# The values products of a dilated attention stage: one product of 128 columns for both halves of v, two PSUM banks for each block

## The chip, the cores and the metric

The kernel runs on one core of a Trainium2 chip. The core has a matrix engine (TensorE, PE in the profile, with its weight loads shown as PEld), a vector engine (VectorE, DVE), an activation engine (ScalarE, ACT), a general engine (GpSimd, POOL) and a queue that issues transfers (SyncE, SP). The matrix engine writes only into PSUM, a memory of eight banks of 512 float32 values for each of 128 partitions; DVE and ACT read results out of it, POOL does not in this kernel. The metric is the device time of one execution in microseconds, lower is better, as the median of several runs.

## The reference, cut to what matters

An encoder layer runs over two sequences, of 2048 and of 512 tokens. A projection of the normed input gives queries, keys and values for a 2-D neighbourhood attention and for three dilated attentions (dilations 1, 4 and 16), and gates. The change is in the dilated attentions: each query sees its neighbours within half a window in a subsequence of stride `dil`.

```python
def band_attention(q, k, v, half):      # per subsequence, blocks of queries
    ...
    s = jnp.einsum('bnqhd,bnkhd->bnhqk', qp, kw).astype(jnp.float32) / math.sqrt(dh)
    s = jnp.where(ok[:, None], s, NEG)
    m = jnp.max(s, axis=-1, keepdims=True)
    p = jnp.exp(s - m)
    den = jnp.sum(p, axis=-1, keepdims=True)
    o = jnp.einsum('bnhqk,bnkhd->bnqhd', (p / den).astype(v.dtype), vw)
    lse = (m + jnp.log(den))[..., 0].transpose(0, 1, 3, 2)
    ...
for gi, (win, dil) in enumerate(((128, 1), (512, 4), (2048, 16))):
    o, lse = dilated_attention(q, k, heads(parts[base + 2]), win, dil)
wts = jax.nn.softmax(jnp.stack(lses), axis=0)
o_b = jnp.einsum('gblh,gblhd->blhd', wts, jnp.stack(outs))
```

There are 8 heads of 64 values. All inputs are float32.

## The kernel before

**Two halves for each number.** Float32 accuracy is had from 16-bit products: a number is split into a high and a low 16-bit part, and a product of two numbers is made as high by low, high by high and low by high, all added in PSUM. Projections, scores and values all work so.

**Stages.** The dilated stage comes first, then the neighbourhood stage, then the gates, then the output. In the dilated stage the kernel goes through 60 tiles of 128 tokens, 20 for each dilation. For each tile it makes three projections (q, k, v), each of 24 products of 512 columns into one of four PSUM banks `proj` (`bank`, line 699). ACT copies q or k out of the bank (`qk<-proj`) and squares it out of the bank (`sq<-proj`, after which the bank is free), DVE adds up the squares (`q_ssq`), POOL turns and scales the result, ACT and DVE or POOL split it into halves (`qs`), and a transfer turns it. ACT and DVE split v into `dv`, in which the 64 high and the 64 low parts of a head stand side by side.

**A block of attention** (`dil_block`, line 1533) is 128 or 64 queries against one or two tiles of 128 keys. There are 66 blocks: 30 with 256 keys and 36 with 128. The eight heads are dealt to units: with 256 keys four units of two heads (0 and 2, 1 and 3, 4 and 6, 5 and 7), with 128 keys two units of four heads (the even ones, the odd ones). Units go in pairs. For each unit PE makes scores into one of two banks `s`; DVE adds the mask and takes each row's maximum in one instruction (`e<-s,cmask`, printed as ISA in the lists of order below) and writes the maximum into the block's tile `osb`; ACT turns it into a shift (`neg<-osb`), makes the exponential and its sum; ACT or DVE round it to `p`, DVE or POOL make the low part; a transfer turns p into `pT`.

**The values** (`pump`, line 854) come when a unit's `pT` has landed, in the order of the units. For each head and tile of keys there are three products with 64 columns of v, each with its own weight load of a 128-column piece of `pT`: high p by low v, high p by high v, low p by high v. With 256 keys that is 48 products for a block, with 128 keys 24. All eight heads of a block, 64 columns each, go into one bank `o`; the kernel has two such banks, so that consecutive blocks alternate. After the last unit `finish` copies 512 columns from the bank to `osb` on ACT, gives the bank back, and `store` writes `osb` to memory and frees the block's q and v tiles. The neighbourhood stage uses the same `pump` and the same two banks.

**What sets the order.** The program is written out by a planner in the kernel itself. It keeps a clock (`Clock`) and a queue for each engine, books a cost for each instruction (`mm`, `act`, `vec`, `pool`), and emits what is ready next. `copy` and `either` choose ACT or DVE, DVE or POOL, by which would be done first by the booked costs. PE's order is the projections, with scores and values put in at the moment when the planner's clock says that their inputs are there and, for the values, that a bank `o` has been granted (`Slots`). Each engine then executes its own list in this order.

Of the kernel before, what the change touches and what calls it, by code (L numbers as in the profile page):

```python
# [18 lines left out]
ALU = mybir.AluOpType  # L19
# [62 lines left out]
M_S = 0.0  # L82
# [92 lines left out]
class Slots:  # L175
# [89 lines left out]
class Enc:  # L265
# [588 lines left out]
    def pump(self):  # L854

        while self.values and "ready" in self.values[0]:
            u = self.values[0]
            if u["first"] and "o" not in u["st"]:
                u["st"]["o"] = None

                def granted(u=u):
                    u["st"]["o"] = self.new("o", [128, 512])
                    self.pump()

                self.S["o"].take(granted)
                return
            if u["st"].get("o") is None or len(u["v"]()) < u["n"] // 128:
                return
            self.values.popleft()
            m, nch, nh = u["m"], u["n"] // 128, len(u["hs"])  # L870
            for i, h in enumerate(u["hs"]):
                out = u["out"](i)
                for j in range(nch):
                    v = u["v"]()[j][:, h]
                    ph, pl = (u["pT"][:, c * nch * nh + i * nch + j, :m] for c in range(2))
                    self.mm(out[:m], ph, v[:, 1], j == 0, False)
                    self.mm(out[:m], ph, v[:, 0], False, False)
                    self.mm(out[:m], pl, v[:, 0], False, j == nch - 1)
            self.S["pT"].give(u["pT"])
            if "last" in u:  # L880
                self.clk.then(u["last"])
# [231 lines left out]
    def na_group(self, seq, g):  # L1113
# [50 lines left out]
        def unit(c, hs):  # L1164
# [4 lines left out]
            u = {"m": 128, "n": n, "hs": hs, "first": hs[0] == 0, "v": lambda: st["v"], "sc": self.sc[0], "st": st,  # L1169
                 "bm": bm}  # L1170

            def scores(s):
# [19 lines left out]
                return st["den"][:, hs[j]:hs[j] + 1]  # L1192

            def out(j):
                return st["o"][:, 64 * hs[j]:64 * hs[j] + 64]

            def finish():
                osb = st["osb"] = self.new("osb", [128, 256], pool=self.N["osb"])
                st["parts"] = self.N["osb"].tile([128, 2, 256], FP16, name=f"oparts{S['osb'].index(osb)}", bufs=1)
                rden = self.T.tile([128, 4], F32, name="rden")  # L1200
                self.vec("reciprocal", rden, st["den"])
                self.vec("tensor_tensor", osb.rearrange("p (h d) -> p h d", d=64),
                         st["o"][:, 0:256].rearrange("p (h d) -> p h d", d=64),
                         rden.unsqueeze(2).to_broadcast([128, 4, 64]), op=ALU.mult)
                S["o"].give(st["o"])
                S["vc"].give(st["vt"])
                clk.then(high)

# [324 lines left out]
    def dil_block(self, R, srcs, m, q, ks, vs, mask, free):  # L1533
# [6 lines left out]
        def unit(h0):  # L1540

            hs = tuple(range(h0, h0 + 2 * nh, 2))

            def scores(s):
                return [(s[:m, n * j:n * j + n], q(), self.ring[:, :, ks()], h, 8, m) for j, h in enumerate(hs)]

            def osb():
                if "osb" not in st:
                    st["osb"] = self.new("osb", [128, OW])
                return st["osb"]  # L1550

            def finish():
                self.act(st["osb"][:m, 0:512], st["o"][:m])
                S["o"].give(st["o"])
                clk.at(clk.done + M_S, store)

            def store():
                p0 = 0
                for t, cnt in srcs:
                    cnt = min(cnt, m)  # L1560
                    self.dma(self.rows_of(self.ob_d[gi], t, cnt, d), st["osb"][p0:p0 + cnt])
                    p0 += cnt
                S["osb"].give(st["osb"])
                free()
                self.blocks_left -= 1
                if self.blocks_left == 0:
                    self.dil_done.signal()

            u = {"m": m, "n": n, "hs": hs, "first": h0 == 0, "st": st, "v": vs, "scores": scores, "sc": self.sc[1],
                 "scored": lambda: None,  # L1570
                 "mask": lambda j: mask, "topped": lambda: None, "out": lambda j: st["o"][:, 64 * hs[j]:64 * hs[j] + 64],
                 "mx": lambda: osb()[:m, 512 + h0:511 + h0 + 2 * nh:2], "den": lambda j: osb()[:m, 520 + hs[j]:521 + hs[j]]}
            if hs[-1] == 7:
                u["last"] = finish
            return u

# [599 lines left out]
```

## Time and profile before

| what | value |
|---|---|
| median of 3 runs | 2861.87 us (2861.65 to 2867.31) |
| profiled execution, its own time | 2864.63 us |
| its span, first to last instruction | 2862.8 us |
| mean granted TensorE clock | 0.971 of full speed |
| busy: PE, DVE, ACT, POOL | 93%, 55%, 47%, 52% of the span |
| dilated stage | from the start to about 1263 us |
| neighbourhood stage | about 1263 to 1800 us |
| gates and output | from about 1800 us |

The table's shares are means over stages that differ. Two stretches of the dilated stage are read apart in the rows below: 140 to 870 us, in which the blocks of dilations 1 and 4 end (39 evacuations of `o`), and 870 to 1263 us. A PE instruction's length in the profile holds its passage through the array, and consecutive ones overlap; what a product takes of PE's time is read from the distance between starts. "idle before" of a group is the time that the engine stood still ahead of those instructions, with what ended it.

### The profile page before, as it was taken

How to read it: one execution, taken by the hardware profiler on the slowest of the kernel's cores; microseconds unless marked ns; L12 is line 12 of the kernel's file. 1: busy time of each engine (PE TensorE's matmuls, PEld its weight loads, DVE VectorE, ACT ScalarE, POOL GpSimd, SP SyncE). 2: the span in 40 equal slices, each digit the busy share in tenths (PEclk: the TensorE clock that was granted, in tenths of full speed). 3: DMA queues.
4: the chain of work that ended last, by engine and by line, in shares of the span. 5: the costliest groups of instructions: out<-in, count | busy, mean ns of one | idle time of the engine just before them, and what ended most of it. 6: DMA issues, size and time to landing. Idle time of an engine off the chain costs nothing.

```text
span 2862.8 us, 55914 instructions
## 1 busy us (share of the span) xinstructions
PE 2675.4 (93%) x20841; PEld 1788.6 (62%) x20841; DVE 1576.5 (55%) x3670; ACT 1334.6 (47%) x3561; POOL 1474.7 (52%) x1991
## 2 busy tenths in 40 slices
PE   5998989989999999999898886899999999999999
PEld 2444444444444444455455554889999999999887
DVE  7777666775655764557676687332145444454111
ACT  5666666665666665656666667221123121122010
POOL 4987768677778888756676664000012121131110
PEclk9999999999999999999999996899999999999999
DMA  7999886766675755588998897332144344353443
GB/s 208 223 214 195 176 196 110 158 127 119 114 121 114 156 114 115 98 224 182 192 226 190 180 206 169 85 71 75 45 129 159 109 128 133 110 172 118 148 139 110
DMA packets 808017, 419.21 MB, mean 146 GB/s; under 512 B 689728, under 2 KB 734400, under 8 KB 801344
## 3 DMA queue, kind: packets, MB, share of 16 engines
q1 hardware_dynamic: 807744, 415.63, 62.9%
q8 instruction: 163, 2.67, 0.4%
q14 instruction: 110, 0.90, 0.1%
HBM read 171.72 MB, written 79.13 MB: 88 GB/s over the span
## 4 chain that ended last, share of the span: by engine, by line
PE 65%; DVE 9%; POOL 8%; DMA 7%; ACT 6%; issue 4%; SPq 1%; DVEq 0%; POOLq 0%; ACTq 0%
PE proj L352 54%; PE s L352 10%; POOL qk L377 4%; DMA pT<-p 4%; PE o L352 2%; DVE p L365 2%; ACT e L360 2%; DVE e L365 2%; POOL sq L377 2%; DMA qn<-qs 1%; POOL q_t L377 1%; ACT sq L360 1%; DVE wm L365 1%; DVE q_ssq L365 1%; ACT qk L360 1%
## 5 line engine op out<-in xcount | busy, mean ns | idle before, releaser
L352 PEld LDWEIGHTS <-hb 128*128 128x128 f16 x6240 | 591.6, 99 | 684.6 <-issue 124.8
L352 PE MATMUL proj<-wt,hb 128*128 128x512 f16 (+2 forms) x3360 | 688.0, 357 | 26.1 <-ACT sq L360 18.0
L352 PE MATMUL proj<-wu,hb 128*128 128x512 f16 x2880 | 668.4, 385 | 45.1 <-ACT sq L360 30.5
L360 ACT ACTIVATE sg<-proj,wi 128x256 f32<-128x256 f32 x240 | 113.1, 473 | 639.3 <-PE proj L352 629.7
L360 ACT ACTIVATE e<-e,neg,sc 128x256 f32<-128x256 f32 (+4 forms) x688 | 393.4, 574 | 8.4 <-DVE neg L365 4.5
L352 PE MATMUL proj<-hb,wt 128*128 128x256 f16 x2760 | 313.7, 274 | 5.0 <-DMA hb<-htd 2.1
L352 PEld LDWEIGHTS <-pT 128*128 128x128 f16 (+1 forms) x4560 | 227.7, 102 | 139.1 <-DMA pT<-p 64.1
L352 PEld LDWEIGHTS <-wt 128*128 128x128 f16 x2760 | 269.3, 98 | 39.4 <-issue 4.0
L377 POOL TENSOR_TENSOR qk<-qk,sq 128x512 f32<-128x512 f32 (+1 forms) x141 | 183.9, 1304 | 196.2 <-DVE qk L365 100.7
L365 DVE TENSOR_TENSOR p<-e,p 128x512 f16<-128x512 f32 (+2 forms) x278 | 248.1, 893 | 63.4 <-ACT p L360 59.6
L377 POOL TENSOR_TENSOR sq<-qk,gcs 128x256 f32<-128x256 f32 x240 | 191.4, 818 | 135.6 <-DVE q_ssq L365 128.9
L365 DVE TENSOR_TENSOR qk<-s,sg 128x256 f32<-128x256 f32 x160 | 67.7, 424 | 348.1 <-PE s L352 345.6
L352 PE MATMUL s<-hb,wt 128*128 128x256 f32 x1880 | 246.9, 285 | 0.0
L352 PE MATMUL proj<-hb,kT 128*128 128x256 f16 x1920 | 228.2, 276 | 5.2 <-ACT sg L360 2.7
L352 PEld LDWEIGHTS s<-hb,wt 128*128 128x128 f32 x1880 | 231.2, 189 | 0.9
L377 POOL TENSOR_TENSOR hb<-sg,hb 128x256 fp32r<-128x256 f32 x65 | 54.0, 831 | 341.3 <-ACT hb L360 341.3
L365 DVE CUSTOM_DVE_ANT_0 e<-s,cmask 128x256 f32<-128x256 f32 (+2 forms) x528 | 154.3, 344 | 107.1 <-PE s L352 90.2
L352 PEld LDWEIGHTS <-kT 128*128 128x128 f16 x1920 | 184.4, 99 | 30.5 <-DVE kT L365 3.5
L365 DVE CAST p<-e 128x512 f16<-128x512 f32 (+2 forms) x182 | 120.1, 660 | 131.4 <-ACT e L360 109.5
L377 POOL TENSOR_TENSOR qk<-qk,q_y 128x512 f32<-128x512 f32 x160 | 179.2, 1124 | 5.2
L377 POOL TENSOR_TENSOR qk<-qk,gcs 128x512 f32<-128x512 f32 x120 | 167.0, 1391 | 9.4
L352 PE MATMUL proj<-wv,hb 128*128 128x512 f16 x660 | 156.6, 383 | 8.3 <-ACT sq L360 6.9
(181 smaller groups left out, 3774.9 us busy)
## 6 DMA issues: line engine op xcount, KB each, us to landing
hb<-htd SPq DMA_DIRECT2D x40, 1024.0 KB
wr<-in_w_in SPq DMA_DIRECT2D x132, 256.0 KB
obd<-osb SPq DMA_DIRECT2D x50, 264.0 KB
hd<-xs SPq DMA_DIRECT2D x20, 512.0 KB
htd<-hb SPq DMA_DIRECT2D x10, 1024.0 KB
mad<-qk SPq DMA_DIRECT2D x40, 256.0 KB
e<-obd SPq DMA_DIRECT2D x40, 256.0 KB
sq<-mad SPq DMA_DIRECT2D x40, 256.0 KB
```

What stands on the lines that cost most here:

```text
L352: self.nc.tensor.matmul(out, a, b, start=start, stop=stop, **kw)
L360: self.nc.scalar.activation(out, x, func, **kw)
L365: getattr(self.nc.vector, ins)(out, *a, **kw)
L377: getattr(self.nc.gpsimd, ins)(out, *a, **kw)
```

## The change

In the dilated stage, high p now meets the low and the high part of v in one product: the 128 columns of a head in `dv` are taken whole, and the result is 128 columns wide, 64 of high p by high v and 64 of high p by low v. Low p by high v follows with 64 columns and is added to the first half. So a head and tile of keys takes two products and two weight loads in place of three. Four heads of 128 columns fill a bank, and a block of eight heads takes both banks `o`. With 256 keys the first two units fill one bank and the last two the other; with 128 keys each unit writes to both. When the last odd unit of a bank has been done, ACT copies the second halves (256 columns) to `osb`, DVE adds the first halves out of the bank, and the bank is given back; after both, the block is stored. The neighbourhood stage keeps its products and one bank for a block.

```diff
@@ pump @@
-            if u["first"] and "o" not in u["st"]:
-                u["st"]["o"] = None
...
+            o = u["st"].setdefault("o", {})
+            for b in u["banks"]:
+                if b not in o:
+                    o[b] = None
+
+                    def granted(o=o, b=b):
+                        o[b] = self.new("o", [128, 512])
+                        self.pump()
+
+                    self.S["o"].take(granted)
+                    return
+                if o[b] is None:
+                    return
...
-                    self.mm(out[:m], ph, v[:, 1], j == 0, False)
-                    self.mm(out[:m], ph, v[:, 0], False, False)
-                    self.mm(out[:m], pl, v[:, 0], False, j == nch - 1)
+                    if u["wide"]:
+
+                        self.mm(out[:m], ph, v.rearrange("p x d -> p (x d)"), j == 0, False)
+                        self.mm(out[:m, 0:64], pl, v[:, 0], False, j == nch - 1)
+                    else:
...
@@ dil_block @@
+            banks = sorted({h // 4 for h in hs})
+
...
             def finish():
-                self.act(st["osb"][:m, 0:512], st["o"][:m])
-                S["o"].give(st["o"])
-                clk.at(clk.done + M_S, store)
+                for b in banks:
+                    out = st["osb"][:m, 256 * b:256 * b + 256].rearrange("p (h d) -> p h d", d=64)
+                    o = st["o"][b][:m].rearrange("p (h x d) -> p h x d", x=2, d=64)
+                    self.act(out, o[:, :, 1])
+                    clk.then(add, b, out, o[:, :, 0])
+
+            def add(b, out, o):
+                self.vec("tensor_tensor", out, out, o, op=ALU.add)
+                S["o"].give(st["o"][b])
+                st["left"] = st.get("left", 2) - 1
+                if st["left"] == 0:
+                    clk.at(clk.done + M_S, store)
...
-            if hs[-1] == 7:
+            if hs[-1] % 2:
                 u["last"] = finish
```

Over the whole program the lists of instructions differ in this: 2304 products of 64 columns become 768 of 128 and 768 of 64, with 768 weight loads fewer; ACT's 66 copies of 512 columns become 132 of 256; DVE has 132 additions of 256 columns more. The planner's choices move a little too: DVE rounds 10 pieces of p more and ACT 10 fewer (8 of 128x512), ACT makes 12 shifts `neg` of dilated units more and DVE 12 fewer, POOL makes 8 low parts of p more.

**DVE where a block ends and the next one's scores begin**, some 700 us into the stage. `q_ssq` is the sum of squares of a projection, `dv` the low part of v, `qs` and `p` halves, the tile behind `o` in a row is a bank of values, and the ISA row is the mask and maximum of the next block's first unit. Before:

```order
L365 CAST p1_8735<-e1_8693 128x512
L365 TENSOR_TENSOR qs0_8723<-qk2_8519,qs0_8723 128x512
L365 TENSOR_REDUCE q0_ssq_8760<-sq1_8727 128x8
L365 TENSOR_REDUCE q1_ssq_8819<-sq0_8799 128x8
L365 ISA e0_8859,osb0_8860<-s0_8838,cmask_302 128x256
```

Now:

```order
L365 TENSOR_TENSOR p1_8460<-e1_8421,p1_8460 128x512
L365 TENSOR_REDUCE q2_ssq_8491<-sq0_8479 128x8
L365 TENSOR_TENSOR osb0_8130<-osb0_8130,o1_8392 128x256
L365 TENSOR_TENSOR osb1_8313<-osb1_8313,o0_8482 128x256
L365 SCALAR_TENSOR_TENSOR dv0_8557<-proj0_7670,dv0_8557 128x8x64
L365 TENSOR_TENSOR osb1_8313<-osb1_8313,o1_8538 128x256
L365 ISA e0_8605,osb0_8606<-s0_8588,cmask_302 128x256
```

Three additions of two blocks stand ahead of the next block's mask and maximum, where before there were none.

**ACT at the same place.** `osb<-o` is the evacuation, `neg` the shift for the next block's first unit, which needs DVE's maximum. Before:

```order
L360 ACTIVATE sq0_8799<-proj0_8731 128x512
L360 ACTIVATE q1_y_8821<-q1_ssq_8819,wi4_976 128x8
L360 ACTIVATE q1_y_8821<-q1_y_8821,lnq_184 128x8
L360 ACTIVATE neg0_8861<-osb0_8860,sc1_316 128x2
L360 ACTIVATE neg1_8866<-osb0_8860,sc1_316 128x2
L360 ACTIVATE e0_8859,osb0_8860<-e0_8859,neg0_8861,sc1_316 128x256 x2
L360 ACTIVATE e1_8865,osb0_8860<-e1_8865,neg1_8866,sc1_316 128x256 x2
L360 ACTIVATE osb1_8591<-o1_8743 128x512
```

Now:

```order
L360 ACTIVATE sq0_8479<-proj3_8417 128x512
L360 ACTIVATE osb0_8130<-o1_8392 128x256
L360 ACTIVATE q2_y_8493<-q2_ssq_8491,wi4_976 128x8
L360 ACTIVATE q2_y_8493<-q2_y_8493,lnq_184 128x8
L360 ACTIVATE osb1_8313<-o0_8482 128x256
L360 ACTIVATE dv0_8557<-proj0_7670 128x8x64
L360 ACTIVATE osb1_8313<-o1_8538 128x256
L360 ACTIVATE neg0_8607<-osb0_8606,sc1_316 128x2
L360 ACTIVATE neg1_8612<-osb0_8606,sc1_316 128x2
L360 ACTIVATE e0_8605,osb0_8606<-e0_8605,neg0_8607,sc1_316 128x256 x2
```

The evacuation has moved from behind the next block's shifts and exponentials to ahead of them, in two pieces, with a third of the block before.

**PE where one block's values follow another's**, some 960 us into the stage: the last product of a block, then projections (`proj<-wu,hb`), then the next block's first product. Before (63 projection products lie between the two blocks):

```order
L352 MATMUL o0_12437<-dv1_12033,pT5_12405 128x64
L352 LDWEIGHTS hb0_11935
L352 MATMUL proj2_12499<-wu23_7637,hb0_11935 128x512
...
L352 LDWEIGHTS pT0_12659
L352 MATMUL o1_12776<-dv2_12239,pT0_12659 128x64
```

Now (6 lie between):

```order
L352 MATMUL o1_12132<-dv1_11565,pT5_12068 128x64
L352 LDWEIGHTS hb0_11451
L352 MATMUL proj1_12186<-wu14_6485,hb0_11451 128x512
...
L352 MATMUL proj1_12271<-wu15_6917,hb0_11451 128x512
L352 LDWEIGHTS pT0_12123
L352 MATMUL o0_12261<-dv2_11838,pT0_12123 128x128
L352 LDWEIGHTS pT0_12123
L352 MATMUL o0_12261<-dv2_11838,pT0_12123 128x64
```

Before, the next block writes to the other bank. Now it writes to the banks that the block before it has just filled. Of the 130 times that a bank is used again in the dilated stage, 9, at 6 places, have 15 or fewer projection products between its last product and its next one: 6, 12, 12, 15, 15 and 15. Before, the fewest between two uses of one bank were 51.

## Rows read from the trace of the kernel before

**Rows 1.** Page: busy time, share of the span and instructions of each engine.

```profile
PE 2675.4 (93%) x20841; PEld 1788.6 (62%) x20841; DVE 1576.5 (55%) x3670; ACT 1334.6 (47%) x3561; POOL 1474.7 (52%) x1991
```

**Rows 2.** Windows: stretch, length, busy us of PE, PEld, DVE, ACT, POOL; clock, DMA.

```profile
140.00:870.00 730.00, 666.34 (x5052) 329.64 (x5053) 486.81 (x1188) 471.05 (x1309) 558.69 (x756) 0.97 0.77 151
870.00:1263.00 393.00, 387.01 (x2814) 193.69 (x2813) 223.57 (x635) 232.32 (x718) 319.46 (x474) 0.99 0.62 128
```

**Rows 3.** PE's groups, 140 to 870 us: count | busy us, mean ns | idle before, releasers.

```profile
L352 PE MATMUL proj<-wu,hb 128*128 128x512 f16 x1197 | 284.2, 387 | 29.1 <-ACT sq L360 28.5 <-DVE dv L365 0.3 <-DVE wm L365 0.2
L352 PE MATMUL proj<-wt,hb 128*128 128x512 f16 x780 | 185.5, 386 | 13.4 <-ACT sq L360 11.2 <-DVE dv L365 2.2
L352 PE MATMUL proj<-wv,hb 128*128 128x512 f16 x480 | 114.1, 384 | 8.3 <-ACT sq L360 6.9 <-DVE dv L365 1.3
L352 PE MATMUL o<-dv,pT 128*128 128x64 f16 x1392 | 60.9, 195 | 1.1 <-DMA pT<-p 1.1
L352 PE MATMUL o<-dv,pT 128*64 128x64 f16 x252 | 11.9, 198 | 2.4 <-DMA pT<-p 2.4
L356 PE MATMUL proj<-ident,wm 128*1 128x128 f32 x5 | 1.5, 292 | 5.8 <-ACT sq L360 5.8
```

**Rows 4.** The same, 870 to 1263 us.

```profile
L352 PE MATMUL proj<-wu,hb 128*128 128x512 f16 x1253 | 283.6, 380 | 2.0 <-ACT sq L360 2.0
```

**Rows 5.** Waits, 140 to 870 us: engine <- releaser: us in total, times, longest.

```profile
ACT neg L360 <- DVE osb L365: 124.5, 97, 6.7
...
PE proj L352 <- ACT sq L360: 46.7, 23, 5.8
...
PE proj L356 <- ACT sq L360: 5.8, 3, 2.3
```

**Rows 6.** Tiles qk and osb, 140 to 870 us: count, ns min/median/max, first and last start.

```profile
L360 ACT ACTIVATE qk<-proj x69: 570/577/597, 140.1 to 865.9; 128x512 f32<-128x512 f32 x69
...
L360 ACT ACTIVATE osb<-o x39: 570/576/598, 161.0 to 867.4; 128x512 f32<-128x512 f32 x29, 64x512 f32<-64x512 f32 x10
```

**Rows 7.** Timeline of PE: start us, us, what, x how many in a row.

```profile
701.23 1.46 PE L352 MATMUL proj<-wu,hb 128*128 128x512 f16 x6
702.52 0.51 PE L352 MATMUL o<-dv,pT 128*128 128x64 f16 x12
702.87 0.81 PE L352 MATMUL proj<-wu,hb 128*128 128x512 f16 x3
...
704.16 0.51 PE L352 MATMUL o<-dv,pT 128*128 128x64 f16 x12
...
706.55 0.56 PE L352 MATMUL o<-dv,pT 128*64 128x64 f16 x12
707.05 2.76 PE L352 MATMUL proj<-wt,hb 128*128 128x512 f16 x12
```

**Rows 8.** Page: weight loads of the attention's values, whole span.

```profile
L352 PEld LDWEIGHTS <-pT 128*128 128x128 f16 (+1 forms) x4560 | 227.7, 102 | 139.1 <-DMA pT<-p 64.1
```

**Rows 9.** ACT's groups, whole span: evacuations of 512 and of 256 columns.

```profile
L360 ACT ACTIVATE osb<-o 128x512 f32<-128x512 f32 x54 | 31.4, 582 | 24.2 <-PE o L352 24.1
L360 ACT ACTIVATE v<-proj 128x256 f16<-128x256 f32 x40 | 15.0, 374 | 21.2 <-DMA vd<-v 20.1 <-PE proj L352 1.0
L360 ACT ACTIVATE osb<-o 64x512 f32<-64x512 f32 x12 | 6.9, 576 | 0.0
```

**Rows 10.** DVE's group of the same form as the new additions, whole span.

```profile
L365 DVE TENSOR_TENSOR osb<-o,rden 128x256 f32<-128x256 f32 x40 | 17.0, 424 | 14.4 <-PE o L352 11.1
```

**Rows 11.** POOL's dearest subtraction, 100 to 1200 us.

```profile
L377 POOL TENSOR_TENSOR p<-e,p 64x512 f16<-64x512 f32 x3 | 10.9, 3636 | 1.3 <-DVE p L365 1.3
```

**Rows 12.** Timelines of PE and ACT: a block's last products, its evacuation; another's evacuation.

```profile
985.09 0.51 PE L352 MATMUL o<-dv,pT 128*128 128x64 f16 x12
...
991.71 0.58 ACT L360 ACTIVATE osb<-o 128x512 f32<-128x512 f32 x1
...
704.72 0.60 ACT L360 ACTIVATE osb<-o 128x512 f32<-128x512 f32 x1 [2.46 <-PE o L352]
```

More of the change, by code (lines that the diff above doesn't have):

```diff
@@ L857, in pump @@
             u = self.values[0]
-            if u["first"] and "o" not in u["st"]:
-                u["st"]["o"] = None
[L861 to L867, printed above, removed]
+            o = u["st"].setdefault("o", {})
[9 more added lines that the diff above has]
+                    return
+            if len(u["v"]()) < u["n"] // 128:
                 return
@@ L875, in pump @@
                     ph, pl = (u["pT"][:, c * nch * nh + i * nch + j, :m] for c in range(2))
-                    self.mm(out[:m], ph, v[:, 1], j == 0, False)
-                    self.mm(out[:m], ph, v[:, 0], False, False)
-                    self.mm(out[:m], pl, v[:, 0], False, j == nch - 1)
+                    if u["wide"]:
+                        self.mm(out[:m], ph, v.rearrange("p x d -> p (x d)"), j == 0, False)
+                        self.mm(out[:m, 0:64], pl, v[:, 0], False, j == nch - 1)
+                    else:
+                        self.mm(out[:m], ph, v[:, 1], j == 0, False)
+                        self.mm(out[:m], ph, v[:, 0], False, False)
+                        self.mm(out[:m], pl, v[:, 0], False, j == nch - 1)
             self.S["pT"].give(u["pT"])
@@ L1168, in unit @@
             bm = [bms[(0, 1, 1, 2)[c], h] for h in hs]
-            u = {"m": 128, "n": n, "hs": hs, "first": hs[0] == 0, "v": lambda: st["v"], "sc": self.sc[0], "st": st,
+            u = {"m": 128, "n": n, "hs": hs, "banks": [0], "wide": False, "v": lambda: st["v"], "sc": self.sc[0], "st": st,
                  "bm": bm}
@@ L1194, in out @@
             def out(j):
-                return st["o"][:, 64 * hs[j]:64 * hs[j] + 64]
+                return st["o"][0][:, 64 * hs[j]:64 * hs[j] + 64]
             def finish():
@@ L1202, in finish @@
                 self.vec("tensor_tensor", osb.rearrange("p (h d) -> p h d", d=64),
-                         st["o"][:, 0:256].rearrange("p (h d) -> p h d", d=64),
+                         st["o"][0][:, 0:256].rearrange("p (h d) -> p h d", d=64),
                          rden.unsqueeze(2).to_broadcast([128, 4, 64]), op=ALU.mult)
-                S["o"].give(st["o"])
+                S["o"].give(st["o"][0])
                 S["vc"].give(st["vt"])
@@ L1552, in finish @@
             def finish():
-                self.act(st["osb"][:m, 0:512], st["o"][:m])
-                S["o"].give(st["o"])
-                clk.at(clk.done + M_S, store)
+                for b in banks:
[9 more added lines that the diff above has]
+                    clk.at(clk.done + M_S, store)
             def store():
@@ L1567, in store @@
                     self.dil_done.signal()
-            u = {"m": m, "n": n, "hs": hs, "first": h0 == 0, "st": st, "v": vs, "scores": scores, "sc": self.sc[1],
+            u = {"m": m, "n": n, "hs": hs, "banks": banks, "wide": True, "st": st, "v": vs, "scores": scores, "sc": self.sc[1],
                  "scored": lambda: None,
-                 "mask": lambda j: mask, "topped": lambda: None, "out": lambda j: st["o"][:, 64 * hs[j]:64 * hs[j] + 64],
+                 "mask": lambda j: mask, "topped": lambda: None, "out": lambda j: st["o"][hs[j] // 4][:, 128 * (hs[j] % 4):128 * (hs[j] % 4) + 128],
                  "mx": lambda: osb()[:m, 512 + h0:511 + h0 + 2 * nh:2], "den": lambda j: osb()[:m, 520 + hs[j]:521 + hs[j]]}
-            if hs[-1] == 7:
+            if hs[-1] % 2:
                 u["last"] = finish
```

## The prediction

> **What bounds the kernel now.** I read the page first, then two windows of the dilated stage, then PE's groups in each, the waits, and last single rows. PE is busy for 93% of the span, the others for about half [rows 1]. The two stretches differ [rows 2]: from 140 to 870 us PE is busy for 666.3 of 730 us, from 870 to 1263 us for 387.0 of 393. So in the second nothing but PE's own work counts, and in the first 64 us stand open. What opens them is one thing: PE's projections wait for a bank, and the bank is freed by ACT's `sq`, 28.5 + 11.2 + 6.9 us of such waits, and 5.8 us in the small transposes of the weights' scales [rows 3], in all 52.4 us. The waits view counts 23 for the first 46.7 us and 3 for the other 5.8 [rows 5]: 26 waits, where ACT empties 69 banks of q and k [rows 6]: about 4 in 10 (26/69 = 0.38) come too late. After 870 us such waits make 2.0 us [rows 4]. Why is ACT late? Its longest wait is for DVE: 124.5 us, 97 times, ahead of `neg`, until DVE has a unit's maxima [rows 5]. DVE and ACT wait for each other in turn, each in its fixed order, and PE feels it when four banks don't cover it. No engine of the three is full: DVE is busy for 487 of the 730 us, ACT for 471, POOL for 559 [rows 2].
>
> **What is removed on PE.** A third of the loads and products. What is that worth? Twelve products of 64 columns run from 702.52 to the next product at 702.87 us: 0.35/12 = 29 ns each [rows 7]. Six of 512 columns run from 701.23 to 702.52: 215 ns each. The difference, 186 ns for 448 columns, is 0.415 ns for a column, which is the 2.4 GHz level (0.417), so a product costs 2.3 ns beside its columns. The weight load that each has takes 102 ns as a row [rows 8], but it does not show in the distance: it is done under the products before it. The three products have 192 columns, and so have the two: 128 + 64. The wide one should take 29 + 64 x 0.415 = 55.6 ns, the pair 84.6 in place of 87. That saves 2.4 ns, 768 times: 1.8 us. With 64 queries twelve products take 0.50 us to the next [rows 7], a little more, but these are an eighth of all (288 of 2304), and I take -2 us for the whole. The bounds: no gain at all if the wide product is slower than its columns, and at most a third of the time in which values products keep PE busy (60.9 + 11.9 us in the first stretch [rows 3], 24 us or so after it), about -32 us.
>
> The Trainium skill, "TensorE: Matmul & The Clock Gate", section "Back-to-back issue gap", says that in a stream of pairs of load and product the distance is about 81 ns for 128 columns and about 131 ns for 512. By its 81 ns the pair would take 110 ns in place of 87, and the sum would be some 18 us higher. For 512 columns this trace has 215 ns and not 131, so I don't take it; no row of this trace has a load and a product of 128 full columns.
>
> **What is added on DVE and ACT.** 132 additions of 128 (or 64) x 256. The nearest row is the neighbourhood stage's product out of the same kind of bank, 424 ns [rows 10]: 56.0 us. On ACT 66 evacuations of 582 or 576 ns go (38.3 us), and 132 of 256 columns come, nearest row 374 ns [rows 9], 49.4 us: +11.1 us. All of it lies beside PE, so its cost is what reaches PE by ACT's late `sq`. In the first stretch 39 blocks are evacuated [rows 6]: 78 additions, 33.1 us, and 39 x (2 x 0.374 - 0.58) = 6.6 us on ACT, together 39.7 us. The lowest value is 0: DVE stands still for a third of that stretch. The highest is all 39.7. Between them: an added time can reach PE only at those banks where PE waits already, 0.38 of them, which gives 15.0 us. I take half of that, 7.5 us, because half of each chain of waits is ACT waiting for DVE and half DVE waiting for ACT, and an addition lengthens a queue only where DVE isn't waiting itself. After 870 us I take 0: PE hardly waits there, and ACT and DVE are busy for less than 0.6 of it.
>
> The queues behind the new instructions: an addition waits for ACT's copy, and behind it on DVE stand, as the order shows, `dv` (which frees a projection's bank) or the next block's mask and maximum, for which ACT's `neg` waits. The copies move ahead of the next block's `neg` on ACT, so there the old lateness of the evacuation falls, and that of `neg` grows. The moved choices are small: 10 roundings of p go from ACT to DVE, and POOL gets two more of a dear form, 3.6 us each [rows 11]; POOL has 170 us open in the stretch, and p lands well ahead of its products (PE waits 1.1 + 2.4 us for `pT` [rows 3]). I cost them at 0. `store` comes about 0.8 us later for each block; it holds one of two tiles `osb`, but a block comes every 18 us or so (39 in 730 us [rows 6]), so this too is 0; if the neighbourhood's start hung on the last block it would be those 0.8 us, once.
>
> **The new wait: the bank.** Before, a block had the other bank while its predecessor was read out. Now PE's first product of a block stands behind the addition that empties the bank, in PE's fixed order. The planner leaves 6, 12, 12, 15, 15 and 15 projection products at the six tightest places: 1.3, 2.6, 2.6, 3.2, 3.2 and 3.2 us at 215 ns. How long does emptying take? ACT begins a block's evacuation between 0.05 us (704.16 + 0.51, then 704.72 [rows 7, 12]) and 6.1 us (985.60, then 991.71 [rows 12]) after the last product; over the 66 pairs of such rows the median is 1.5 us. Then come two copies of 0.374 and one addition of 0.424, and DVE may be at something else, which I estimate at 1 us from its busy share of two thirds and its instructions of 0.4 to 1 us: 3.7 us. What is missing at the six places is then 2.4 + 2 x 1.1 + 3 x 0.5 = 6.1 us. The lowest value is 0 (an evacuation that begins at once is over in 1.2 us), the highest that of the latest row at all six (8.3 us of emptying): 7.0 + 2 x 5.7 + 3 x 5.1 = 34 us. I take +6 us.
>
> **The sum.** -2 + 7.5 + 6 = +11.5 us. The terms come from the profiled execution, 2864.63 us with its span of 2862.8; that execution lies 2.8 us above the median, and the terms are differences, so I add them to the median: 2861.87 + 11.5 = 2873 us.
>
> **The rivals.** First, **hidden**: DVE's open third takes the additions in, the planner's covers hold, and only the -2 us are left: 2860 us. For it: the additions are booked by the planner near their cost (0.15 + 256/960 = 0.417), so they are no lateness against its plan; PE in the second stretch feels nothing of a DVE that is late. Against it: 26 waits show that the first stretch has no cover to spare. It decides from the point where the added 39.7 us meet idle DVE and ACT only. This is the rival that ends not slower.
>
> Second, **re-dealt waits**: values move by up to 60 products in PE's order against before, so the 26 waits fall anew. If a quarter of the 52.4 us goes, as the earlier start of evacuations on ACT could do, the time is -13 - 2: 2847 us. For it speaks that 52.4 us are a few single waits of up to 5.8 us, against it that nothing in the change shortens the queue ahead of `sq`.
>
> Third, **the bank becomes the bound**: late emptying as in the dearest row at all tight places, and the additions reach PE at the full 0.38: -2 + 15 + 34 = +47, 2909 us.
>
> Fourth, **loads bound**: each of the 768 loads that go takes its row's 102 ns [rows 8] of PE's time: -78 us, 2784 us. The distances of 29 ns speak against it as flatly as they can. The Trainium skill, "TensorE: Matmul & The Clock Gate", section "LDWEIGHTS (loading the stationary operand)", gives a load's time as its columns over 1.2, in ns, 107 for 128, and so would have -82 us if nothing hid it; the row's 102 ns agree with it as a length, the distance of 29 ns shows that it is hidden.
>
> **How the numbers follow.** Forecast 0.48, hidden 0.28, re-dealt 0.12, bank 0.08, loads 0.04. The likeliest gives 2873 us, in itself 2865 to 2882. The range goes from 2846 us (the re-dealt case) to 2892 us (half way from the sum to the third rival), and leaves out the loads, the bank and some of the tails. 0.2% is 5.7 us, about what a measurement of this kernel can tell from no change. Faster by more: 0.16 (re-dealt, loads). Within: 0.28 (hidden). Slower by more: 0.56 (forecast, bank).
>
> **What would show it.** PE: groups `o<-dv,pT` of 128 and 64 columns with starts 56 and 29 ns apart; busy time in values products hardly changed. If the wide product shows 80 ns or more, the first term is wrong. DVE: 132 additions `osb<-osb,o` near 0.42 us; ACT: 132 copies near 0.37 us. PE's wait for ACT's `sq` from 140 to 870 us at about 60 us in place of 52; if it stays or falls, the second term is wrong. A new group of waits of PE's `o` for DVE's `osb`, about 6 us, at places where the order leaves few projections; if there is none, the third is wrong. The stretches from 1263 us on should be as long as before, to within a few us; a difference there would come from the planner's other order alone and would be none of my terms.

## The result and the profile after

The changed kernel takes 2900.6 us in the median of 4 runs (2897.34 to 2903.12); the kernel before, run beside it, 2864.0 us (2861.65 to 2867.31). The ratio is 1.0119, with a 95% interval of 1.0107 to 1.0132: slower by 36.6 us. 2873 us was foretold, with 2846 to 2892. The sign is right, the size three times too small, and the time lies outside the range.

The page of the changed kernel: the span, and the busy time of each engine (to be read against [rows 1]).

```profile
span 2901.3 us, 54541 instructions
PE 2679.5 (92%) x20073; PEld 1787.1 (62%) x20073; DVE 1622.0 (56%) x3793; ACT 1342.4 (46%) x3629; POOL 1485.3 (51%) x1999
```

No engine became full, so the extra time is time in which engines wait. The windows of the changed kernel over the stretches of [rows 2]: length, busy us of PE, PEld, DVE, ACT, POOL, then clock and DMA.

```profile
140.00:870.00 730.00, 651.09 (x4383) 318.88 (x4383) 501.99 (x1220) 460.55 (x1305) 563.34 (x754) 0.97 0.75 149
870.00:1263.00 393.00, 374.49 (x2505) 183.09 (x2504) 237.21 (x669) 230.21 (x730) 312.65 (x454) 0.98 0.58 119
```

PE stands open for 79 us in the first stretch, where it was 64 us. In the second, where I had seen only PE's own work, it is 18.5 us where it was 6. The granted clock is 0.97 in the first stretch both times and 0.98 for 0.99 in the second, which is worth a few us at the most (an estimate: 0.01 of 393 us is 4 us). How far the program has come, by the start of the nth product of 512 or 256 columns of a projection: product 2400 starts 16.6 us later than before (746.2 against 729.6), product 4560, at the end of the dilated stage, 31.3 us later (1298.1 against 1266.7); the end lies 38.5 us later (2901.3 against 2862.8). So four fifths of the loss arise in the dilated stage.

PE's waits in the changed kernel, 0 to 1300 us: PE, tile and line <- releaser: us in total, times, longest.

```profile
PE proj L352 <- ACT sq L360: 70.2, 43, 6.4
PE proj L356 <- ACT sq L360: 9.8, 4, 5.8
```

In the same stretch of the kernel before these two lines have 48.6 us (24 times) and 5.8 us (3 times): 80.0 now against 54.4. The wait that was foretold to grow did grow, by 25.6 us, and it is most of the 31 us. From 140 to 870 us, the stretch for which some 60 us in place of 52 were foretold, it is 70.6 us:

```profile
PE proj L352 <- ACT sq L360: 60.8, 39, 6.4
PE proj L356 <- ACT sq L360: 9.8, 4, 5.8
```

The instructions on the tile `osb` in the changed kernel, 0 to 1300 us: count, ns min/median/max, first and last start. The second and third line are the new copies and additions. The last three lines say who stood idle for one of these instructions.

```profile
L360 ACT ACTIVATE osb<-o x132: 358/370/402, 110.2 to 1289.9; 128x256 f32<-128x256 f32 x108, 64x256 f32<-64x256 f32 x24
L365 DVE TENSOR_TENSOR osb<-osb,o x132: 399/410/422, 111.5 to 1290.7; 128x256 f32<-128x256 f32 x108, 64x256 f32<-64x256 f32 x24
...
who waited for it (us, times):
  ACT neg L360: 195.5, 144
  DVE osb L365: 41.8, 27
  PE o L352: 1.4, 2
```

The new instructions have the lengths that were taken, 0.37 and 0.41 us. The wait of PE's `o` for the additions, foretold at 6 us, is 1.4 us in 2 places. The additions wait 41.8 us for ACT's copies. Last, PE's timeline with the new products (start, length, what, how many).

```profile
503.86 0.84 PE L352 MATMUL o<-dv,pT 128*128 128x128 f16 x16
506.49 0.50 PE L352 MATMUL o<-dv,pT 128*128 128x128 f16 x8
506.83 1.03 PE L352 MATMUL proj<-wv,hb 128*128 128x512 f16 x4
```

Eight products, four wide and four narrow, run from 506.49 to 506.83: 0.34/4 = 85 ns a pair, as the first term had it (84.6).

### The profile page after: what moved, and what is told of

It reads as the page before. It is cut to its first block, busy times and chain, and to the rows that moved or that the text cites. A ratio compares the mean times of both kernels' runs of the same rounds, so it can differ in the third digit from the quotient of the medians.

```text
span 2901.3 us, 54541 instructions
## 1 busy us (share of the span) xinstructions
PE 2679.5 (92%) x20073; PEld 1787.1 (62%) x20073; DVE 1622.0 (56%) x3793; ACT 1342.4 (46%) x3629; POOL 1485.3 (51%) x1999
## 4 chain that ended last, share of the span: by engine, by line
PE 62%; DVE 10%; POOL 9%; DMA 8%; ACT 6%; issue 4%; SPq 1%; DVEq 0%; ACTq 0%; POOLq 0%
PE proj L352 50%; PE s L352 10%; POOL qk L377 4%; DMA pT<-p 4%; DVE e L365 2%; POOL sq L377 2%; DVE p L365 2%; ACT e L360 2%; PE o L352 2%; DMA wr<-in_w_in 1%; SPq L395 1%; POOL q_t L377 1%; DVE wm L365 1%; DVE wt L365 1%; ACT sq L360 1%
## 5 line engine op out<-in xcount | busy, mean ns | idle before, releaser
L352 PEld LDWEIGHTS <-pT 128*128 128x128 f16 (+1 forms) x3792 | 219.2, 102 | 132.9 <-DMA pT<-p 58.0
L365 DVE TENSOR_TENSOR qs<-qk,qs 128x512 f16<-128x512 f32 (+1 forms) x140 | 125.9, 904 | 79.6 <-ACT qs L360 77.6
```

The costliest lines, as they stand in the source:

```text
L352: self.nc.tensor.matmul(out, a, b, start=start, stop=stop, **kw)
L365: getattr(self.nc.vector, ins)(out, *a, **kw)
```

## The experiments

All are compared with runs of the kernel before on the same chip (2862.6 to 2864.0 us in the median).

Three measures are worked out from each profile. The **distance of blocks** is that of the first maximum of one block from that of the next, from 140 to 870 us. The **hold of osb** goes from a block's first maximum to the end of its last store's issue. The **hold of v** goes from a v projection's last product to the end of DVE's low half of `dv`, after which the bank `proj` is free (the first 43 tiles).

### The work, or its place in the plan?

The first question was whether executing the additions costs the time, or the order that the planner makes when it books them. One kernel leaves the additions out of the changed kernel but keeps its order, its copies and its two banks.

```diff
-self.mm(out[:m], ph, v.rearrange("p x d -> p (x d)"), j == 0, False)
-self.mm(out[:m, 0:64], pl, v[:, 0], False, j == nch - 1)
+...   # three products of 64 columns into out[:m, 0:64]; booked as the two
-self.act(out, o[:, :, 1])
+self.act(out, o[:, :, 0])
-self.vec("tensor_tensor", out, out, o, op=ALU.add)
+self.clk.run("V", 0.15 + size(out) / 960)
```

> The changed kernel in its own order, with all its bookings by the planner and both banks, but without DVE's 132 additions: PE makes the three products of 64 columns as before into the first half of each head's 128 columns, and ACT's 132 copies of 256 columns read that half. (The result is complete.) Theory W, the additions' time on DVE (132 x 0.41 us) is what PE gets to feel: about 2866 us, and the same by theory Q, that the wait of an addition for ACT's copy, with all that stands behind it on DVE, is what PE feels. Theory P, the planner's other order with two banks for a block and an evacuation in two pieces costs the time by itself: about 2900 us.

Measured: 2893.3 us, 1.0106 (1.0091 to 1.0121). Without one addition executed, 30 of the 37 us are there. The windows of this kernel, as above: PE stands open for 77.3 us in the first stretch and 14.6 in the second, nearly as in the changed kernel (78.9 and 18.5).

```profile
140.00:870.00 730.00, 652.70 (x4911) 321.33 (x4911) 477.42 (x1149) 463.36 (x1317) 559.75 (x754) 0.97 0.76 150
870.00:1263.00 393.00, 378.41 (x2738) 186.00 (x2738) 223.81 (x621) 231.81 (x738) 313.26 (x455) 0.99 0.60 119
```

Two kernels give the kernel before two additions for each block, behind ACT's copy: on the block's own tile, and on a constant that nobody waits for.

```diff
 def finish():
     self.act(st["osb"][:m, 0:512], st["o"][:m])
     S["o"].give(st["o"])
-    clk.at(clk.done + M_S, store)
+    clk.then(more)
+def more():
+    for b in range(2):
+        x = st["osb"][:m, 256 * b:256 * b + 256]   # or: self.cmask[...]
+        self.vec("tensor_tensor", x, x, x, op=ALU.max)
+    clk.at(clk.done + M_S, store)
```

> The kernel before, with two more DVE instructions of 128x256 for each block behind ACT's copy of 512 columns (the maximum of a half of osb with itself, which leaves it as it is), booked by the planner; products, banks and copy as before. W and Q: 2890 to 2905 us. P: 2864 to 2870 us.

> As the run before it, in the same order of instructions on every engine, but the two instructions work on a constant tile, so that they wait for nobody. W: the same time as with the wait, 2890 to 2905 us. Q: 2864 to 2872 us. P: 2864 to 2870 us.

Measured: 2896.1 us (1.0118, 1.0101 to 1.0135) and 2896.4 us (1.012, 1.0102 to 1.0138). With the old products and one bank the additions, booked and executed, make 33 of the 37 us, and it is no less when they wait for nothing: the wait of an addition for ACT's copy is not the price.

A control makes the planner book 2 ns in place of 3 for what a product costs beside its columns, so that numbers of the plan change but no work.

```diff
-... / 2400 + 0.003) / share
+... / 2400 + 0.002) / share
```

> A control: the kernel before, in which the planner books 2 ns in place of 3 ns beside the columns of each product, so that the order of all engines moves a little and no instruction is other than before. W and Q: within 6 us of 2864. P in its strong form, any other order can cost or give tens of microseconds: 2850 to 2900, that is more than 10 us away.

Measured: 2860.4 us, 0.9994 (0.9983 to 1.0004). This other plan moves nothing clear of the noise; it is one plan, and doesn't say what every other would do.

Next the two parts of the added work apart, in the kernel before: booked and not executed, and executed without being booked, that is in exactly the order of before. A third kernel is the changed one with the additions executed and not booked.

```diff
 # booked only
-self.vec("tensor_tensor", x, x, x, op=ALU.max)
+clk.run("V", 0.15 + 256 / 960)
 # executed only (the store stays where it was in the plan)
-self.vec("tensor_tensor", x, x, x, op=ALU.max)
+self.nc.vector.tensor_tensor(x, x, x, op=ALU.max)
 # the changed kernel, unbooked
-self.vec("tensor_tensor", out, out, o, op=ALU.add)
+self.nc.vector.tensor_tensor(out, out, o, op=ALU.add)
+clk.done = clk.now
```

> The kernel before in exactly the order of the run with additions behind its copy: the planner books two additions of 128x256 for each block on DVE and lets the block's store wait for them, but no addition is executed; all instructions are those of before. If the order that the planner makes of the bookings costs the time (theory P, now narrowed to: a busier DVE in the plan re-orders all queues, and the new order serves PE's banks worse): 2890 to 2897 us. If the additions' execution costs it (theory W): 2860 to 2870 us.

> The other half: the kernel before in exactly its own order, in which DVE executes two additions' worth of 128x256 for each block behind ACT's copy, and the planner books nothing for them. W: 2890 to 2897 us. P: 2863 to 2870 us.

> The changed kernel, complete, with its wide products, two banks and 132 additions, where the planner books no time for the additions and hands a bank on when ACT's copy is over. P: most of the time comes back, 2863 to 2880 us, since the plan is then nearly that of before but for the banks. If the banks or the evacuation in two pieces cost the time, or W: 2890 us or more; the bank's wait on PE will grow from 1.4 us, by at most some microseconds.

Measured: booked only 2878.7 us (1.0047, 1.0033 to 1.0061), executed only 2879.9 us (1.0048, 1.003 to 1.0066), the changed kernel unbooked 2883.1 us (1.0058, 1.0042 to 1.0074). All three lie between the cases that were expected. In the kernel before, booking alone costs 15 us and execution alone 16 us; together they make the 33 us of the kernel that has both. In the changed kernel the parts don't add up so: unbooked additions save 17.5 us of the 37, additions that are booked and not executed only 7 (2900.6 against 2893.3 us). So the place in the plan costs as much as the work in the one kernel, and more than it in the other.

What does booking move? The block's store comes later, and with it all that the store frees. So that alone:

```diff
-clk.at(clk.done + M_S, store)
+clk.at(clk.done + M_S + 2 * (0.15 + 256 / 960) + LAG_V, store)
```

> The kernel before, in which the planner lets each block's store, and all that it frees (tiles of q, k, v and osb), come 1.2 us later, the time that two additions would take, and books nothing on DVE. If what is freed later makes the worse order: 2885 us or more. If DVE's booked time does: within 8 us of 2863.

Measured: 2887.6 us, 1.0075 (1.0059 to 1.0092). Nothing is added here; each store, and the places that it frees, come 1.18 us later in the plan. That costs 23.6 us. It is more than the 15 us of the kernel with booked additions, whose stores come later by at least as much; so what a plan does beside the one thing that was meant can be worth 9 us. PE's waits of this kernel from 140 to 870 us:

```profile
PE proj L352 <- ACT sq L360: 59.2, 33, 5.8
```

against 46.7 us and 23 times in [rows 5], and 60.8 us and 39 times in the changed kernel: the line of the changed kernel's loss, made by a later store alone.

### Which place does the store hold?

`store` gives back the tile `osb` (two) and the block's q, k and v tiles (six `dq`, four `dk`, three `dv`). Who waits for them, and how does that reach PE? A v projection keeps its bank `proj` until a tile `dv` is free. In the kernel before the hold of v is 46.2 us in the mean, where q and k hold theirs for 2.7 us; at one tile in some 20 us (43 in the first 870), v projections sit on 2.3 of the four banks, and q and k share the rest. By this reading that is why PE waits for `sq` there. In the changed kernel the hold of v is 50.3 us. Four kernels take that up: q, k and v tiles given back in the plan at the block's last product instead of after the store's landing, in both kernels; a fourth tile `dv`, paid for with the sixth `dq`, in the kernel before; and both.

```diff
 def finish():      # in the changed kernel only after the block's last unit
+    clk.done = clk.now
+    free()
...
 def store():
...
-    free()
 # a fourth tile
-("dv", 3)
+("dv", 4)
-NDQ = 6
+NDQ = 5
```

> New theory V: a projection's v lies in one of the four banks of the projections until one of the three tiles dv is free; the planner frees a dv tile when its block's store has landed, so whatever puts the store later (two additions, a copy in two pieces) holds v's banks longer, and PE is left with fewer banks and waits for ACT's sq on the next one. In the trace of before v's bank is held for 46 us on the mean over the first 43 tiles, q's and k's for 2.7. This run is the kernel before with one thing other: tiles of q, k and v are freed in the plan when the block's last product is done, some 4 us earlier. V: PE's waits shrink, 2835 to 2850 us, with v's banks held 4 us less. Rival P' (any plan other than that of before is worse, since its constants were tuned for it): 2864 to 2900 us.

> The changed kernel with the same one thing other: tiles of q, k and v freed in the plan at the block's last product, before the copies and the additions. V: most of what was lost comes back, 2865 to 2880 us. P': 2895 to 2910 us.

> The kernel before with four tiles dv in place of three, paid for by one tile less of turned queries (five in place of six); all else as before. V: v's bank is held shorter by up to the 20 us of a tile, PE's waits for ACT's sq fall from 54 us to under 30, 2820 to 2845 us. P': 2864 to 2900 us.

> Both: four tiles dv, five of queries, and all freed at the block's last product. V: 2815 to 2840 us. P': 2864 to 2900 us.

Measured: the kernel before with the early free 2843.2 us (0.9928, 0.9911 to 0.9945), with the fourth tile 2827.3 us (0.9872, 0.9857 to 0.9887), with both 2816.2 us (0.9834, 0.9819 to 0.985). PE's wait for `sq` from 140 to 870 us in this order:

```profile
PE proj L352 <- ACT sq L360: 25.3, 12, 4.9
```

```profile
PE proj L352 <- ACT sq L360: 17.0, 13, 6.9
```

```profile
PE proj L352 <- ACT sq L360: 6.9, 8, 1.7
```

The wait goes as the places come free earlier, with the hold of v (44.1, 36.1 and 30.3 us). But the changed kernel with the early free takes 2911.6 us (1.0165, 1.0146 to 1.0183), 11 us more than without. That was a plain miss: the `dv` tiles are not the only place in the loop. In this kernel a `dv` tile lies unread for 2.8 us between its last product and its next writing, where the changed kernel has 9.9 us; and the gain is lost elsewhere, since the life of a tile, from its writing to its last product, grows from 58.1 to 66.4 us. The block may have had another place to wait for, which the next four runs ask: the hold of `osb` is 31.3 us, the next block's first maximum in that tile follows 8.1 us later, and half of the sum, 19.7 us, is the distance of blocks (28.0, 8.3 and, as half of the sum, 18.1 us in the kernel before with the early free).

### The tiles osb

Four kernels on that place: `osb` given back in the plan at the store's issue, in the changed kernel with the early free and in the fastest kernel above; a third tile `osb`, paid for with the sixth `dq`, in the changed kernel with the early free and without.

```diff
 # given back at issue (the transfer is still waited for where the tile is written)
+clk.done = clk.now
 S["osb"].give(st["osb"])
 # a third tile
-S["osb"] = Slots(self.clk, 2)
+S["osb"] = Slots(self.clk, 3)
-NDQ = 6
+NDQ = 5
```

> The changed kernel with the early free of the q, k and v tiles, and with the tile osb given back in the plan when the block's store is issued instead of when it has landed (the chip still waits for the landing where it has to). In the changed kernel with the early free of q, k and v alone (2911.6 us), a block holds its tile osb 31.3 us from its first maximum to the issue of its store, and the next block's first maximum follows 8.1 us later; half of the sum, 19.7 us, is the distance of the blocks. In the kernel before with the same early free it was 28.0 and 8.3 us, 18.1 in half. Theory W (two tiles osb are the next place that a block waits for, and the two copies and two additions of a block keep it longer): the 8.1 us fall to 5 to 6 us, the blocks come 18.4 to 18.8 us apart, and the time is 2855 to 2885 us. Rival X (the looser plan puts more work of the next tiles ahead of the additions on ScalarE and VectorE, whatever place is given back): no gain or a loss, 2905 to 2925 us.

> The changed kernel with the early free of q, k and v and three tiles osb in place of two (five dq tiles in place of six pay for the room). Theory W: a block no longer waits for a tile osb, so the time falls to 2850 to 2885 us and the blocks come 18.2 to 18.8 us apart, though each block may hold its tile longer than 31 us. Rival X: 2905 to 2925 us. Should it stay near 2911 while the run with osb given back early falls, the fifth dq tile is what is missing.

> The changed kernel with three tiles osb (and five dq tiles), and q, k, v freed at the store's landing as written. If the tiles osb alone hold back the changed kernel, the time falls to 2865 to 2880 us. If the dv tiles hold it first and osb only behind them (theory W as it stands: a dv tile lies unread for 9.9 us of its 68 us cycle in the changed kernel, 2.8 us with the early free), it gains little: 2885 to 2905 us.

> The kernel before with four dv tiles, five dq tiles, the early free of q, k, v (2816.2 us with these), and osb given back in the plan at the store's issue. Theory W: with the dv tiles loosened the tiles osb bound this one (a block holds its tile 28.1 us, the next follows 7.2 us later, 17.7 us a block), so it gains: 2790 to 2810 us. Rival X says nothing of this kernel, which has no additions; if osb is not a bound the time stays at 2812 to 2820 us.

Measured: the third tile with the early free 2834.9 us (0.9908, 0.9891 to 0.9924), without it 2854.0 us (0.9974, 0.9962 to 0.9986). Both gain more than was expected, and both are faster than the kernel before. The rival, by which a looser plan only piles work ahead of the additions, is out by its own forecast (2905 to 2925 us): the early free that cost 11 us with two tiles `osb` and six `dq` brings 19 us with three and five.

Given back at issue: 2888.9 us in the changed kernel (1.0099, 1.0081 to 1.0116), 23 us better than without it and just outside the expectation; in the fastest kernel 2881.5 us (1.0069, 1.0054 to 1.0084), 65 us worse, a clear miss. Two waits, 140 to 870 us, in the one and in the other, show what came in: DVE's wait for the store, which neither kernel has without this edit, and PE's scores behind it (2.5 and 10.7 us without).

```profile
DVE e L365 <- DMA obd<-osb: 59.6, 15, 5.8
PE s L352 <- DVE osb L365: 24.0, 20, 5.0
```

```profile
DVE e L365 <- DMA obd<-osb: 85.1, 26, 8.6
PE s L352 <- DVE osb L365: 55.8, 35, 5.8
```

The maximum of the next block now stands at the head of DVE's queue until the store has landed, and all that DVE has behind it waits too. A place that is given back before it is free turns a wait of the planner, which lets other work pass, into a wait of an engine, which doesn't. In the changed kernel the earlier place is still worth more than that wait, in the fastest kernel not; why, no run shows. The early free of q, k and v was better off, since their readers are done by then.

Two doubts: does the third tile help the kernel before as much, and is it the missing `dq` tile that helps?

```diff
 # the kernel before: third osb, five dq
-S["osb"] = Slots(self.clk, 2)
+S["osb"] = Slots(self.clk, 3)
-NDQ = 6
+NDQ = 5
 # the changed kernel: five dq, nothing else
-NDQ = 6
+NDQ = 5
```

> The kernel before with three tiles osb in place of two and five dq tiles in place of six. The same two edits brought the changed kernel from 2900.6 to 2854.0 us. Theory W' (the later store of the changed kernel cost it what it did because two tiles osb were too few; before, a block held its tile 26.3 us against 27.4, and waited less for one): the kernel before gains clearly less than 47 us, 2835 to 2858 us, and the distance of the two kernels shrinks from 37 to under 20 us. Rival (the third tile loosens both kernels alike, and the additions cost what they cost): 2808 to 2825 us, the distance stays at 30 to 45 us.

> The changed kernel with five dq tiles in place of six and nothing else: the control of every run here that paid for a third osb or a fourth dv tile with a dq tile. If the osb and dv tiles gave those gains, this stays at 2890 to 2920 us. If the fifth dq tile itself gave them (it holds back the q tiles, and so how many tiles the plan keeps in flight), this falls to 2850 to 2870 us.

Measured: the kernel before 2869.7 us (1.0022, 1.0011 to 1.0034), no gain at all, where both expectations had one; the changed kernel with five `dq` 2878.2 us (1.0048, 1.0029 to 1.0067), between the two cases. So of the 47 us that both edits bring to the changed kernel, 22 come with five `dq` tiles and 24 with the third `osb`. With the same tiles, three `osb` and five `dq`, the changed kernel is the faster one, 2854.0 against 2869.7 us. The same change of products costs 37 us on one set of tiles and gains 16 on another.

The second row of the table is the control.

| kernel | us | distance of blocks | hold of osb | hold of v |
|---|---|---|---|---|
| before | 2864.0 | 18.5 | 26.3 | 46.2 |
| before, 2 ns booked for 3 | 2860.4 | 18.5 | 27.0 | 45.3 |
| before, executed only | 2879.9 | 19.0 | 28.1 | 47.2 |
| before, booked only | 2878.7 | 18.9 | 26.8 | 48.0 |
| before, store later | 2887.6 | 19.2 | 27.1 | 49.3 |
| changed | 2900.6 | 19.2 | 27.4 | 50.3 |
| changed, five dq | 2878.2 | 18.9 | 27.1 | 47.3 |
| changed, early free | 2911.6 | 19.7 | 31.3 | 51.0 |
| before, early free | 2843.2 | 18.3 | 28.0 | 44.1 |
| changed, three osb, five dq | 2854.0 | 17.8 | 28.6 | 44.2 |
| the same, early free | 2834.9 | 17.3 | 32.8 | 36.5 |
| before, three osb, five dq | 2869.7 | 18.3 | 27.0 | 45.5 |
| before, four dv, five dq, early free | 2816.2 | 17.7 | 28.1 | 30.3 |

## Why the prediction was wrong

**Term 1, PE: right.** The pair takes 85 ns, as it was worked out from the 64- and 512-column distances of [rows 7]. The 81 ns for 128 columns (the Trainium skill, "TensorE: Matmul & The Clock Gate", section "Back-to-back issue gap"), which was not taken, isn't seen here: 85 - 29 = 56 ns. (The 18 us that the prediction adds to its sum by those 81 ns, an estimate, count from no saving; from its own -2 us they are 20.) The new pieces of `pT` still take a load each, and as with the 64-column products no load shows in the distance.

**Term 3, the bank: too large.** 1.4 us in 2 places, where 6 us was taken and 34 us was the bound. The covers of 12 and 15 products that stood at most of the six places were enough.

**Term 2, the additions: the lengths and the growing wait right, the size met by luck in one order.** The new instructions take what was put down for them, and PE's wait for `sq` grows. What executing them costs goes by the order: 7 us in the changed kernel's own (2900.6 against 2893.3 us, hardly clear of the noise, and with the products of before on PE), 16 us in that of the kernel before (9 to 19 by the interval of the ratio), 17 us in the order made with bookings (2896.1 against 2878.7 us). The 7.5 us were worked out as a share of past waits (0.38 of 39.7 us, then half), and that says who was late, not how much further each becomes late. The 0 after 870 us failed: PE stands open for 18.5 us there, where it was 6, and for 14.6 us with no addition executed.

**The step that failed most: the 0 for the later store.** "`store` comes about 0.8 us later for each block; it holds one of two tiles `osb`, but a block comes every 18 us or so (39 in 730 us [rows 6]), so this too is 0". The other order was put at nothing with it, and the runs showed the reverse: the changed kernel's order costs 30 of the 37 us without one addition executed, and a store that is merely 1.18 us later in the plan costs the kernel before 23.6 us, with PE's wait for `sq` up from 46.7 to 59.2 us. The step named one of the places that hang on the store and left out the tiles of q, k and v; and it read a block's distance as slack, without asking how long a block holds its tile.

It holds it for 26.3 us, the next block's first maximum in it comes 10.8 us later, and two tiles in turn make that 37.1/2 = 18.5 us, the distance. If the 10.8 us could not shrink, the 1.1 us that a block keeps its tile longer in the changed kernel (27.4 us) would move the distance by 0.55 us, and 66 blocks by 36 us. That is an estimate, near the 31 us that the dilated stage lost, but the table speaks against it: the control holds its tile for 27.0 us and the kernel before with the early free for 28.0 us, and their blocks come 18.5 and 18.3 us apart. So part of the 10.8 us is free time, and a longer hold of `osb` alone doesn't set the distance.

Which place carries the loss is shown in part. In the changed kernel a third `osb`, beside five `dq`, is worth 24 us. In the kernel before it brings nothing, with the tiles `dv` held nearly as long as before (hold of v 45.5 us), while an earlier free of q, k and v brings 20 us, or a fourth `dv` beside five `dq` 35 us; in the changed kernel the early free alone costs 11 us, and beside a third `osb` it brings 19. That two sets of places, `osb` and `dv`, hang on the same store and are both just enough is a reading of these runs, and not shown: no run makes one of them late without the other.

**What I asked too late.** "Why is ACT late?" was answered with ACT and DVE waiting for each other [rows 5]. The other half of the answer is in no wait that the view names: a v projection sits on a bank `proj` because its tile isn't there yet. That shows as PE waiting for `sq`, the release of another bank. One would have seen it by following a bank from the last v product to DVE's `dv`.

**The rivals.** Hidden, re-dealt and loads are refuted by the time. The bank as the bound came nearest in its time (2909) and is wrong in its cause. The stretches from 1263 us on, which "should be as long as before, to within a few us", were a little off too: 7 us more are lost there (38.5 - 31.3); in the control, with another plan, products of those stretches start up to 19 us earlier than in the kernel before, and the end lies 3.5 us earlier. I take it for the order, and that is argued, not shown.

**What stays open.** How the loss divides between the tiles `osb` and `dv` is not settled, as said. Why five `dq` tiles in place of six bring the changed kernel 22 us is not settled; it holds back q tiles and so how many tiles of a later block are under way, but no run tells that from a luckier order. The kernel before was not run with five `dq` alone, so in the gain of the fourth `dv` the share of the `dq` tile isn't known. Both sets loosened at once in the kernel before (three `osb`, early free, five `dq`) was not run. Each kernel is one plan, and single edits of the plan may be worth some us either way.

**Versions that beat both.** The kernel before with four `dv`, five `dq` and the early free: 2816.2 us. The changed kernel with three `osb`, five `dq` and the early free: 2834.9 us.

## What to carry to other kernels

Before a later release is costed at nothing, list every place that hangs on it, and run the later release alone: here 1.18 us in the plan cost 23.6 us. The hold of a place plus the gap to its next use, over the number of places, is always the distance of the rounds; a longer hold costs its share only as far as the gap can't shrink, and a control shows whether it can. Work and its place in a plan are two things to measure: not executing the additions gave back 7 us of 37 in the changed kernel's order. A wait for one consumer's bank can be made by another consumer that sits on the other banks, so follow each bank from its last write to its release. And a place given back too early to the planner becomes a wait in an engine's queue, with everything behind it.
